# The start and the first passage between sets of a gated MLP kernel: DMAs on one queue, sums and casts in another order

## The chip, the cores and the metric

One core of a Trainium2 chip runs the kernel. TensorE (PE) multiplies, VectorE (DVE), ScalarE (ACT) and GpSimd (POOL) work on elements, SyncE (SP) issues DMAs, and so can ACT and POOL. Each of them runs its own instructions in order and waits on semaphores. The metric is the time of one execution in microseconds (us). Shorter is better.

## The reference

```python
# x [16, 256, 512], w1 [512, 4096], w2 [2048, 512], all float32
h = x @ w1
gate, value = np.split(h, 2, axis=-1)
h = np.maximum(gate, 0) * value
return (h @ w2).astype(np.float32)
```

That is two matrix products on 4096 rows, with a gate (columns 0 to 2047 of the first product) and a value (columns 2048 to 4095) between them.

## The kernel before

All products run in float16 with float32 accumulation. A small judge on the data's size decides whether this fast way's output stands or a general float32 way (a branch) runs. The branch isn't taken here, and the profile shows the fast way alone.

**Sets and blocks.** The 4096 rows are worked in four *sets* (s = 0 to 3) of 1024 rows, two halves of 512. A set's first product is made in 16 *blocks* (jb) of 128 hidden columns, gate and value together. Its second product, `mm2`, follows as a stream of 224 matmuls, of which the first 20 are put between the last matmuls of block 15 and the last 8 between the first blocks of the next set.

**Seven products instead of eight.** Each block is a 2x2 product of matrices of halves, made in Winograd's form of Strassen's scheme: seven products P1 to P7 on the quarters and on sums of quarters, at the cost of adding beforehand. Three families of sums are needed.
- *Of x*: x_S1 to x_S4 from x_A1 and x_A2 (the halves of a set's rows, transposed). DVE makes them (`x_sum`, line 448).
- *Of the weights*: T1 to T4. For w1 they are the tiles `wt`, one for each of six chunks of blocks (blocks 0-1, 2-3, 4-5, 6-7, 8-11, 12-15). POOL makes those of blocks 4 to 15 (`w1_ops`, line 158) while set 0 runs, DVE those of blocks 0 to 3 behind set 0's x sums, since set 0's blocks 0 to 3 are made in plain form (`Plain`). For w2 they are the tiles `v_T1` to `v_T4`: SP copies a quarter of w2 into each (line 529), and POOL then adds to it by an accumulating DMA (`add_w2`, line 161).
- *Of g*, the gated result of the first product: S1 to S4 (`g_sum`, line 271). S1 needs g's lower half of rows from block h and block h + 8, S3 needs blocks 0 to 7 only; S2 is made from S1, and S4 from S2. In set 0 POOL makes S3 at blocks 11 to 14, and three quarters of S1 after the last block; DVE makes the last quarter of S1, and S2 and S4. In later sets POOL makes one 512-wide piece after each block, and DVE the last two of each sum.

In `mm2` the order is P1 and P2 (from g itself) for three blocks of rows, and then P5 (S1), P6 (S2), P3 (S4), P7 (S3) and P4 (from g) for two of them, and so on. ACT and DVE evict: DVE's are lines 312 and 317.

**How x arrives.** Set 0's x is read by DMA: the first half as float32 on SP (tile `xf`, in the memory of g's S1), the second half as float16 on POOL (`xh`, in S2). TensorE transposes them. For sets 1 to 3 `cast_x(s)`, a DMA on POOL, writes the set's rows as float16 to DRAM (`x16`), and four DMA transposes on SP (line 384) bring them to x_A1 and x_A2. The tiles x_A exist once, so that the transposes wait for the last matmul that reads the set before, and for the cast. They and two fetches of plain rows for the judge are written behind a set's blocks, ahead of the output stores on the same queue.

**The start.** SP issues the two parts of x's first half (called x0 and x1 in the prediction), ACT the gate and the value part of w1's columns for blocks 0 and 1 (w0 and w1 there). ACT and DVE cast the latter to float16. A POOL copy into `gate` waits for x0 and holds back all of POOL's DMAs until then. POOL then fetches w1's columns of blocks 2 and 3, the second half of x, and the other columns. TensorE runs eight idle matmuls on a zeroed tile (`warm`) meanwhile.

Where the order is set: the program is written in the order in which each engine takes its instructions. For set 0 the list on POOL is, after the fetches, `w1_ops` with the fetches of w2 between them, the accumulates, and then what the loop over the time slots adds (`plan`, at block jb's product P1):

```python
if n == "P1" and s == 1 and jb < 2:
    cast_x(2 + jb)
...
if n == "P1" and s == 0 and jb in (11, 12, 13, 14):
    g_sum(nc.gpsimd, go, "S3", 2 * jb - 22, 2 * jb - 20)
    if jb == 12:
        add_w2("T4", "T2")
    if jb == 14:
        cast_x(1)
```

Of the kernel before, what the change touches and what calls it, by code (L numbers as in the profile page):

```python
# [9 lines left out]
F32, F32R, F16 = dt.float32, dt.float32r, dt.float16  # L10
# [6 lines left out]
P = 128  # L17
# [8 lines left out]
HALF = 256  # L26
NHC = 8
# [72 lines left out]
def fast_way(ctx, tc, x2, w1, w2, out2, flag):  # L100

    nc = tc.nc
# [5 lines left out]
    NJ = H // P  # L108
# [4 lines left out]
    wpool = ctx.enter_context(tc.tile_pool(name="wpool", bufs=1))  # L113
# [8 lines left out]
    w1_v = w1.rearrange("(e p) (g j) -> p e g j", p=P, g=2)  # L122
    w2_v = w2.rearrange("(hc p) n -> p hc n", p=P)
    x_v = x2.rearrange("(s b p) d -> s p b d", p=P, b=2 * NB)
# [4 lines left out]
    wr = [wpool.tile([P, 4, 2, n * P], F16, name=f"wr{c}") for c, (_, n) in enumerate(CHUNKS)]  # L129
    wt = [wpool.tile([P, 4, 2, n * P], F16, name=f"wt{c}") for c, (_, n) in enumerate(CHUNKS)]  # L130
    w2_h = [wpool.tile([P, NJ, HALF], F16, name=f"w2_{i}") for i in range(2)]
    v_t = {n: wpool.tile([P, NHC, HALF], F16, name=f"v_{n}") for n in ("T1", "T2", "T3", "T4")}
    x16 = {s: dpool.tile([SET, D], F16, name=f"x16_{s}") for s in range(1, NS)}

    NX = 2 * 2 * NB * NS
# [12 lines left out]
    V = {f"B{k + 1}{n + 1}": w2_h[n][:, k * NHC:(k + 1) * NHC] for k in range(2) for n in range(2)}  # L148
# [4 lines left out]
    def w1_ops(eng, jb, n):  # L153
        for t in TURNS:
            w1_one(eng, jb, n, *t)

    def w1_one(eng, jb, n, m, a, b, o):
        eng.tensor_tensor(W(m, jb, n), W(a, jb, n), W(b, jb, n), op=o)

    def add_w2(m, v):  # L160
        nc.gpsimd.dma_start(out=V[m], in_=V[v], accum_op=ADD)

    warm = tmp.tile([P, 2, TH], F32, name="warm", tag="tmp")
    warm_b = warm.rearrange("p a t -> p (a t)").bitcast(F16)
    nc.vector.memset(warm[:, 0], 0.0)
    ident = {t: wpool.tile([P, P], t, name=f"ident{k}") for k, t in enumerate((F32, F16))}
    gate = wpool.tile([P, 1], F32, name="gate")

# [5 lines left out]
    def x_tiles():  # L174
        o = {f"A{h}": xpool.tile([P, 4, TH], F16, name=f"x_A{h}") for h in (1, 2)}
        for h in (1, 2):
            for k in (1, 2):
                o[f"A{h}{k}"] = o[f"A{h}"][:, 2 * k - 2:2 * k]
        for n in ("S1", "S2", "S3", "S4"):
            o[n] = xpool.tile([P, 2, TH], F16, name=f"x_{n}")  # L180
        return o
# [86 lines left out]
    def g_sum(eng, go, n, h0, h1):  # L268
        for m, i0, i1, op in SUMS:
            if m == n:  # L270
                eng.tensor_tensor(go[n][:, h0:h1], go[i0][:, h0:h1], go[i1][:, h0:h1], op=op)  # L271
# [69 lines left out]
    def advance(stream, n):  # L341
        for _ in range(n):
            if stream is None or next(stream, 0) == 0:
                return
# [5 lines left out]
    def fetch_w2(i):  # L350
        ks, n = slice(i // 2 * NHC, i // 2 * NHC + NHC), i % 2
        nc.gpsimd.dma_start(out=w2_h[n][:, ks], in_=w2_v[:, ks, n * HALF:(n + 1) * HALF])

    def cast_x(s):
        nc.gpsimd.dma_start(out=x16[s], in_=x2[s * SET:(s + 1) * SET, :])

    def g_tiles():
        g = gpool.tile([P, NJ, SET], F16, name="g")
        gs = {n: gpool.tile([P, NHC, TH], F16, name=f"g_{n}") for n in ("S1", "S2", "S3", "S4")}
        return g, g_ops(g, gs)  # L360

    g, go = g_tiles()
    xf = go["S1"].rearrange("p a t -> p (a t)").bitcast(F32).rearrange("p (b d) -> p b d", b=NB)
    xh = go["S2"][:, :NB]
    wl = g[:, NJ - 4:].rearrange("p a t -> p (a t)").bitcast(F32).rearrange("p (e g j) -> p e g j", e=4, g=2)
# [16 lines left out]
    def turn_by_dma(s, o, h):  # L382
        for k in range(2):
            nc.sync.dma_start_transpose(out=o[f"A{h + 1}{k + 1}"], in_=x16[s][h * TH:(h + 1) * TH, k * 256:k * 256 + 256])
# [7 lines left out]
    def fetch_rows(s, q):  # L392
        rows[s, q] = xpool.tile([P, 2, D], F16, name=f"xn{q % 2}")
        nc.sync.dma_start(out=rows[s, q], in_=x16[s][q * 256:(q + 1) * 256].rearrange("(b p) d -> p b d", p=P))
# [3 lines left out]
        t = rows[s, b // 2][:, b % 2] if s else (xf, xh)[b // NB][:, b % NB]  # L398
        look(t[:, i % 2 * 256:i % 2 * 256 + 256], 4 * NB * s + i, 256)

    for b in (0, 2):
        nc.sync.dma_start(out=xf[:, b:b + 2], in_=x_v[0, :, b:b + 2])
    for g_ in range(2):
        nc.scalar.dma_start(out=wl[:, :, g_], in_=w1_v[:, :, g_, :2 * P])
    for t in ident.values():
        make_identity(nc, t)
    nc.gpsimd.tensor_copy(out=gate, in_=xf[:, 0, :1])
# [38 lines left out]
    def x_sum(o):  # L446
        n, i0, i1, op = sums.pop(0)
        nc.vector.tensor_tensor(o[n], o[i0], o[i1], op=op)
# [16 lines left out]
    def look_w1(i):  # L465
        c, o = place[i // 2 * 2]
        look(wr[c][:, :, i % 2, o * P:(o + 2) * P], NX + i, 1024)

    def look_w2(i):
        look(w2_h[i % 2][:, i // 2 * 4:i // 2 * 4 + 4].rearrange("p h n -> p (h n)"), NW + i, 1024)  # L470
# [26 lines left out]
    for s in range(NS - 1):  # L497
        for i in range(8):
            f = (lambda i=i + 8 * s: look_w1(i)) if s < 2 else (lambda i=i: look_w2(i))
# [11 lines left out]
    for s in range(NS):  # L511
        if s:
            g, go = g_tiles()
        first = NPLAIN if s == 0 else 0
        blocks = {jb: Block(xo, g, jb) for jb in range(first, NJ)}
        plan = {jb * PERIOD + at: (jb, n) for jb in blocks for n, at in SLOT.items()}
        last = NJ * PERIOD
        stream = mm2_stream(s, go)
        if s == 0:
            w1_ops(nc.gpsimd, 4, 2)  # L520
            fetch_w2(0)
            fetch_w2(1)
            w1_ops(nc.gpsimd, 6, 2)
            fetch_w2(2)
            fetch_w2(3)
            w1_ops(nc.gpsimd, 8, 2)
            w1_ops(nc.gpsimd, 10, 2)
            for m, v in (("T1", "B11"), ("T3", "B12"), ("T2", "B22"), ("T4", "B21")):
                nc.sync.dma_start(out=V[m], in_=V[v])
            for t in TURNS:  # L530
                w1_one(nc.gpsimd, 12, 4, *t)
                if t[0] == "T2":
                    add_w2("T1", "B12")
                    add_w2("T3", "B22")
            add_w2("T2", "T1")
        for at in range(first * PERIOD, last + PERIOD):
            if at in plan:
                jb, n = plan[at]
                if n == "P1" and s == 1 and jb < 2:
                    cast_x(2 + jb)  # L540
                if n == "P1" and s and jb in (4, 8):
                    fetch_rows(s, 1 + jb // 4)
                if n == "P1" and s == 0 and jb in (11, 12, 13, 14):
                    g_sum(nc.gpsimd, go, "S3", 2 * jb - 22, 2 * jb - 20)
                    if jb == 12:
                        add_w2("T4", "T2")
                    if jb == 14:
                        cast_x(1)
                getattr(blocks[jb], n)()
                if n == "P5":  # L550
                    for f in LOOKS.get((s, jb), ()):
                        f()
                if n == "P4" and s:
                    if jb < NHC:
                        g_sum(nc.gpsimd, go, "S3", jb, jb + 1)
                    elif jb < NJ - BY_DVE:
                        for m in ("S1", "S2", "S4"):
                            g_sum(nc.gpsimd, go, m, jb - NHC, jb - NHC + 1)
            elif at >= last:
                advance(stream, 4)  # L560
            else:
                advance(prev, 4)
        if s == 0:
            for h in (0, 2, 4):
                g_sum(nc.gpsimd, go, "S1", h, h + 2)
            g_sum(nc.vector, go, "S1", 6, 8)
            for m in ("S2", "S4"):
                for h in (0, NHC // 2):
                    g_sum(nc.vector, go, m, h, h + NHC // 2)
        else:  # L570
            for m in ("S1", "S2", "S4"):
                g_sum(nc.vector, go, m, NHC - BY_DVE, NHC)
        done = 20
        if s + 1 < NS:
            xo = x_tiles()
            for h in range(2):
                turn_by_dma(s + 1, xo, h)
            for q in range(2):
                fetch_rows(s + 1, q)
            advance(stream, 100)  # L580
            sums = list(SUMS)
            for _ in SUMS:
                x_sum(xo)
            if s == 0:
                w1_ops(nc.vector, 0, 2)
                w1_ops(nc.vector, 2, 2)
            advance(stream, MM2 - TAIL - 100 - done)
        else:
            advance(stream, MM2)
        prev = stream  # L590
# [29 lines left out]
```

## Time and profile before

| | us |
|---|---|
| median of 3 runs (lowest, highest) | 324.63 (324.35, 325.35) |
| the profiled execution | 325.27 |
| its span, first to last instruction | 323.5 |
| TensorE busy | 305.7 |
| DVE busy | 211.5 |
| ACT busy | 189.2 |
| POOL busy | 151.5 |

A row of the order of time has the start in us from the span's begin, the length in us, the engine, the line of the kernel, the operation, what it writes and reads (tiles by name, buffer numbers left out, so that `g_S` is any of g's sums and `x_S` any of x's), and how many instructions are merged. In brackets stands the engine's idle time before it, and what ended it. "SPq" and "POOLq" are DMA issues. A row of waits has the waiting engine and line, what it waited for, the total us, the number and the longest. A row of windows has the stretch, the busy time of PE, its weight loads, DVE, ACT and POOL with their counts, the granted TensorE clock, the mean busy share of the 16 DMA engines, and GB/s. "PE" with one digit for each of 40 slices shows the busy share of each 8.09 us in tenths. "DMA to landing" is the time from issue to landing, shortest, median and longest of the DMAs of one line in a stretch.

### The profile page before, as it was taken

What the parts mean: (1) busy time and instruction counts of PE and PEld (TensorE: products, weight loads), DVE (VectorE), ACT (ScalarE), POOL (GpSimd) and SP (SyncE); (2) the same over time, 40 slices, a digit from 0 to 9 for tenths busy, and PEclk for the clock granted to TensorE, in tenths of its full rate; (3) what the DMA queues carried; (4) which work ended last, traced back from release to release, by engine and by line L of the source; (5) the groups of instructions that cost most, each with busy time, mean ns of one, the idle gap of its engine ahead of it and who ended that gap; (6) DMA issues with size and microseconds to landing.
All of it is one profiled execution on the core that took longest, in us unless ns stands there. A gap on an engine that the chain in (4) does not pass through costs nothing.

```text
span 323.5 us, 5143 instructions
## 1 busy us (share of the span) xinstructions
PE 305.7 (95%) x1867; PEld 183.0 (57%) x1867; DVE 211.5 (65%) x329; ACT 189.2 (58%) x450; POOL 151.5 (47%) x137
## 2 busy tenths in 40 slices
PE   6999999978929999999999999999999999999993
PEld 3654444557814444448885444447885444447882
DVE  1377888895074888887424888888324888888311
ACT  2347766536607676673866766763876766763230
POOL 3879999980000433897000434897000334898000
PEclk9999999999969999999999999999999999999997
DMA  7999979499951101006422101007422101000123
GB/s 240 179 202 204 230 217 213 78 197 195 169 221 65 33 2 32 0 3 131 136 104 88 32 0 34 0 0 116 149 99 97 32 2 32 0 2 0 67 79 120
DMA packets 33593, 30.74 MB, mean 95 GB/s; under 512 B 13888, under 2 KB 27968, under 8 KB 33472
## 3 DMA queue, kind: packets, MB, share of 16 engines
q0 software_dynamic: 10704, 11.54, 21.9%
q1 hardware_dynamic: 21664, 17.70, 18.2%
q10 hardware_dynamic: 1200, 1.18, 1.2%
q8 instruction: 15, 0.25, 0.3%
q14 instruction: 10, 0.08, 0.1%
HBM read 24.12 MB, written 11.53 MB: 110 GB/s over the span
## 4 chain that ended last, share of the span: by engine, by line
PE 69%; DVE 0%; ACT 0%; issue 0%
PE Y L200 19%; PE X L200 13%; PE W L200 13%; PE Y L282 11%; PE W L282 6%; PE X L282 6%; ACT pv L323 0%; DVE pv L317 0%; DVE o L312 0%; PE W L485 0%
## 5 line engine op out<-in xcount | busy, mean ns | idle before, releaser
L271 POOL TENSOR_TENSOR g_S<-g 128x512 f16<-128x512 f16 (+1 forms) x49 | 64.0, 1332 | 133.4 <-DVE g L237 131.4
L200 PEld LDWEIGHTS <-wt 128*128 128x128 f16 x480 | 46.9, 98 | 56.9 <-issue 4.1
L200 PE MATMUL X<-x_A,wr 128*128 128x512 f16 x240 | 71.7, 381 | 0.2 <-ACT Y L207 0.2
L200 PE MATMUL Y<-x_S,wt 128*128 128x512 f16 x240 | 71.4, 379 | 0.0
L227 DVE SCALAR_TENSOR_TENSOR cc<-W,pu 128x512 f32<-128x512 f32 x60 | 41.5, 692 | 37.2 <-ACT pu L221 36.4
L200 PEld LDWEIGHTS <-wr 128*128 128x128 f16 x360 | 35.1, 98 | 41.3 <-issue 0.5
L207 ACT COPY Y<-X 128x512 f32<-128x512 f32 x60 | 34.2, 570 | 39.4 <-PE X L200 21.4
L282 PEld LDWEIGHTS <-g_S 128*128 128x128 f16 x512 | 49.6, 98 | 9.5 <-DVE g_S L271 1.9
L282 PEld LDWEIGHTS <-g 128*128 128x128 f16 x384 | 37.9, 99 | 14.8 <-issue 6.5
L221 ACT ACTIVATE pu<-Y 128x512 f32<-128x512 f32 x60 | 35.9, 598 | 14.3 <-PE Y L200 14.3
L228 DVE SCALAR_TENSOR_TENSOR g<-X,cc 128x512 f16<-128x512 f32 x60 | 41.5, 691 | 2.3
L237 DVE SCALAR_TENSOR_TENSOR g<-Y,cc 128x512 f16<-128x512 f32 x60 | 40.9, 682 | 2.8 <-PE Y L200 2.8
L233 DVE SCALAR_TENSOR_TENSOR cc<-Y,pu 128x512 f32<-128x512 f32 x60 | 40.9, 681 | 0.1
L214 ACT ACTIVATE pu<-W 128x512 f32<-128x512 f32 x60 | 36.1, 602 | 0.1
L200 PE MATMUL W<-x_S,wt 128*128 128x512 f16 x120 | 36.0, 382 | 0.0
L200 PE MATMUL Y<-x_A,wt 128*128 128x512 f16 x120 | 35.5, 377 | 0.2 <-DVE cc L233 0.2
L200 PE MATMUL W<-x_S,wr 128*128 128x512 f16 x120 | 35.7, 379 | 0.0
L282 PE MATMUL Y<-v_T,g_S 128*128 128x256 f16 x256 | 30.8, 273 | 0.5 <-DVE g_S L271 0.5
L282 PE MATMUL X<-w,g 128*128 128x256 f16 x256 | 31.2, 272 | 0.0
L312 DVE SCALAR_TENSOR_TENSOR o<-W,pv 128x256 f32<-128x256 f32 x16 | 6.7, 424 | 31.6 <-PE W L282 31.6
L323 ACT ACTIVATE pv<-Y 128x256 f32<-128x256 f32 x16 | 6.1, 382 | 32.0 <-PE Y L282 32.0
L282 PE MATMUL Y<-v_T,g 128*128 128x256 f16 x128 | 17.1, 281 | 5.9 <-DVE pv L317 5.9
(67 smaller groups left out, 317.6 us busy)
## 6 DMA issues: line engine op xcount, KB each, us to landing
out_dram<-o SPq DMA_DIRECT2D x16, 256.0 KB, 2.2
out_dram<-pv SPq DMA_DIRECT2D x15, 256.0 KB, 2.0
x<-in_x_dram POOLq DMA_DIRECT2D x3, 1024.0 KB, 9.5
xn<-x SPq DMA_DIRECT2D x12, 256.0 KB, 3.0
wr<-in_w_dram POOLq DMA_DIRECT2D x4, 512.0 KB, 13.9
w<-in_w_dram POOLq DMA_DIRECT2D x4, 512.0 KB, 10.9
v_T<-w SPq DMA_DIRECT2D x4, 512.0 KB, 4.9
wr<-in_w_dram POOLq DMA_DIRECT2D x6, 256.0 KB, 8.6
```

The costliest lines, as they stand in the source:

```text
L200: nc.tensor.matmul(ps, W(wn, self.jb)[:, b], self.xo[xn][:, b, :], start=fresh and b == 0, stop=b == 1, skip_group_check=True)
L207: nc.scalar.copy(out=self.Y, in_=self.X)
L214: nc.scalar.activation(self.p5, self.W, COPY, scale=GS)
L221: nc.scalar.activation(self.u2, self.Y, COPY, scale=-GS)
L227: nc.vector.scalar_tensor_tensor(out=self.c12, in0=self.W, scalar=GS, in1=self.u2, op0=MULT, op1=ADD)
L228: nc.vector.scalar_tensor_tensor(out=self.g[:, self.jb, :TH], in0=self.X, scalar=0.0, in1=self.c12, op0=MAX, op1=MULT)
L233: nc.vector.scalar_tensor_tensor(out=self.c22, in0=self.Y, scalar=-GS, in1=self.p5, op0=MULT, op1=ADD)
L237: nc.vector.scalar_tensor_tensor(out=self.g[:, self.jb, TH:], in0=self.Y, scalar=0.0, in1=self.c22, op0=MAX, op1=MULT)
L271: eng.tensor_tensor(go[n][:, h0:h1], go[i0][:, h0:h1], go[i1][:, h0:h1], op=op)
L282: nc.tensor.matmul(ps, go[gn][:, k, b * P:(b + 1) * P], V[vn][:, k, :], start=fresh and k == 0, stop=k == NHC - 1, skip_group_check=True)
L312: nc.vector.scalar_tensor_tensor(out=d["o1"][:, HALF:], in0=d["W"], scalar=1 / GS, in1=d["pu"][:, 1], op0=MULT, op1=ADD)
L323: nc.scalar.activation(d["o2"][:, :HALF], d["Y"], COPY, scale=1 / GS)
```

## The change

It has five parts.
- *Start.* SP issues all four first DMAs, in turn: x0, w0, x1, w1. The idle tile's zeroing is half as wide.
- *w2's sums.* T3 and T2 become the halves of one tile `v_12`. One 1 MB copy from `w2_h[1]` (B12 and B22 side by side) takes the place of two of 0.5 MB, so that SP issues three copies instead of four. T4's accumulate goes from block 12 to block 15.
- *cast_x(1)* goes from block 14 to the place right behind T2's accumulate, ahead of all sums of g.
- *Sums of g in set 0.* POOL makes pieces of S1 and S3 in turn at blocks 11 and 13, and a piece of S1 at block 15. The second half of S3 moves from POOL to the end of DVE's list.
- *Casts of sets 2 and 3* go from set 1's blocks 0 and 1 (P1) to the places behind POOL's S3 pieces of set 1's blocks 1 and 4, which wait for these blocks.

```diff
-    v_t = {n: wpool.tile([P, NHC, HALF], F16, name=f"v_{n}") for n in ("T1", "T2", "T3", "T4")}
+    v_12 = wpool.tile([P, NJ, HALF], F16, name="v_12")
+    v_t = {n: wpool.tile([P, NHC, HALF], F16, name=f"v_{n}") for n in ("T1", "T4")}
+    v_t.update(T3=v_12[:, :NHC], T2=v_12[:, NHC:])
...
-    nc.vector.memset(warm[:, 0], 0.0)
+    nc.vector.memset(warm[:, 0, :HALF], 0.0)
...
-    for b in (0, 2):
-        nc.sync.dma_start(out=xf[:, b:b + 2], in_=x_v[0, :, b:b + 2])
-    for g_ in range(2):
-        nc.scalar.dma_start(out=wl[:, :, g_], in_=w1_v[:, :, g_, :2 * P])
+    for i in range(2):
+        nc.sync.dma_start(out=xf[:, 2 * i:2 * i + 2], in_=x_v[0, :, 2 * i:2 * i + 2])
+        nc.sync.dma_start(out=wl[:, :, i], in_=w1_v[:, :, i, :2 * P])
...
-            for m, v in (("T1", "B11"), ("T3", "B12"), ("T2", "B22"), ("T4", "B21")):
-                nc.sync.dma_start(out=V[m], in_=V[v])
+            for to, v in ((V["T1"], V["B11"]), (v_12, w2_h[1]), (V["T4"], V["B21"])):
+                nc.sync.dma_start(out=to, in_=v)
...
             add_w2("T2", "T1")
+            cast_x(1)
...
-                if n == "P1" and s == 1 and jb < 2:
-                    cast_x(2 + jb)
...
-                if n == "P1" and s == 0 and jb in (11, 12, 13, 14):
-                    g_sum(nc.gpsimd, go, "S3", 2 * jb - 22, 2 * jb - 20)
-                    if jb == 12:
+                if n == "P1" and s == 0 and jb in (11, 13, 15):
+                    h = jb - 11
+                    if h == 4:
                         add_w2("T4", "T2")
-                    if jb == 14:
-                        cast_x(1)
+                    for m in ("S1", "S3")[:2 - h // 4]:
+                        g_sum(nc.gpsimd, go, m, h, h + 2)
...
                         g_sum(nc.gpsimd, go, "S3", jb, jb + 1)
+                        if s == 1 and jb in (1, 4):
+                            cast_x(2 + jb // 4)
...
-            for h in (0, 2, 4):
-                g_sum(nc.gpsimd, go, "S1", h, h + 2)
             g_sum(nc.vector, go, "S1", 6, 8)
             for m in ("S2", "S4"):
                 for h in (0, NHC // 2):
                     g_sum(nc.vector, go, m, h, h + NHC // 2)
+            g_sum(nc.vector, go, "S3", NHC // 2, NHC)
```

POOL's instructions from the accumulates of w2's sums to the end of set 0 and the first of set 1, before. Here `v_T3` etc. are w2's sums, `w2_1` is `w2_h[1]`, `wt5` and `wr5` are w1's sums and raw columns of blocks 12 to 15, `x16_s` what a cast writes, and the number at a name's end a buffer:

```order
L161 DMA v_T3_100<-w2_1_97 128x2048
L158 TENSOR_TENSOR wt5_95<-wr5_89 128x1024
L158 TENSOR_TENSOR wt5_95<-wr5_89,wt5_95 128x1024
L161 DMA v_T2_99<-v_T1_98 128x2048
L271 TENSOR_TENSOR g_S3_114<-g_111 128x1024 x2
L161 DMA v_T4_101<-v_T2_99 128x2048
L271 TENSOR_TENSOR g_S3_114<-g_111 128x1024 x2
L355 DMA x16_1_102<-in_x_dram 32x16384
L271 TENSOR_TENSOR g_S1_112<-g_111 128x1024 x3
L355 DMA x16_2_103<-in_x_dram 32x16384
L355 DMA x16_3_104<-in_x_dram 32x16384
L271 TENSOR_TENSOR g_S3_1051<-g_1048 128x512 x8
```

And with the change:

```order
L160 TENSOR_TENSOR wt5_95<-wr5_89,wt5_95 128x1024
L163 DMA v_12_98<-v_T1_99 128x2048
L357 DMA x16_1_101<-in_x_dram 32x16384
L273 TENSOR_TENSOR g_S1_111<-g_110 128x1024
L273 TENSOR_TENSOR g_S3_113<-g_110 128x1024
L273 TENSOR_TENSOR g_S1_111<-g_110 128x1024
L273 TENSOR_TENSOR g_S3_113<-g_110 128x1024
L163 DMA v_T4_100<-v_12_98 128x2048
L273 TENSOR_TENSOR g_S1_111<-g_110 128x1024
L273 TENSOR_TENSOR g_S3_1048<-g_1045 128x512 x2
L357 DMA x16_2_102<-in_x_dram 32x16384
L273 TENSOR_TENSOR g_S3_1048<-g_1045 128x512 x3
```

The cast of set 1 now stands ahead of every g sum, S1 and S3 take turns with T4's accumulate ahead of the last piece, and two pieces of S3 are gone; the casts of sets 2 and 3 stand behind two and five pieces of set 1's S3.

SP's queue from its first DMA to set 1's transposes, before:

```order
L402 DMA g_S1_112<-in_x_dram 128x2x512 x2
L529 DMA v_T1_98<-w2_0_96 128x2048
L529 DMA v_T3_100<-w2_1_97 128x2048
L529 DMA v_T2_99<-w2_1_97 128x2048
L529 DMA v_T4_101<-w2_0_96 128x2048
L384 DMA_TRANSPOSE x_A1_763<-x16_1_102 128x2x512 x2
L384 DMA_TRANSPOSE x_A2_764<-x16_1_102 128x2x512 x2
```

And with the change, where `g_110` is the memory in g that holds the float32 columns of w1:

```order
L404 DMA g_S1_111<-in_x_dram 128x2x512
L405 DMA g_110<-in_w1_dram 128x4x256
L404 DMA g_S1_111<-in_x_dram 128x2x512
L405 DMA g_110<-in_w1_dram 128x4x256
L530 DMA v_T1_99<-w2_0_96 128x2048
L530 DMA v_12_98<-w2_1_97 128x4096
L530 DMA v_T4_100<-w2_0_96 128x2048
L386 DMA_TRANSPOSE x_A1_760<-x16_1_101 128x2x512 x2
L386 DMA_TRANSPOSE x_A2_761<-x16_1_101 128x2x512 x2
```

The two DMAs of w1's first columns have come from ACT's queue between those of x, and the second copy is twice as long and needs both of `w2_h[1]`'s fetches.

## The prediction

> **What bounds the kernel now.** I read the page first, then the waits, then the order of time around the one place where TensorE stands still.
>
> ```profile
> PE 305.7 (95%) x1867; PEld 183.0 (57%) x1867; DVE 211.5 (65%) x329; ACT 189.2 (58%) x450; POOL 151.5 (47%) x137
> PE   6999999978929999999999999999999999999993
> ```
>
> TensorE (PE) is the bound, and whatever the change wins must come out of the few slices below 9: the start, and slices 9 to 12 (65 to 97 us), which are the passage from set 0 to set 1. The waits name what it waited for there, the second fence on SP's queue:
>
> ```profile
> PE Y L282 <- DVE pv L317: 5.9, 1, 5.9
> DVE x_S L448 <- DMA x_A<-x: 9.2, 1, 9.2
> ```
> ```profile
> SPq L384 <- DMA x<-in_x_dram: 26.3, 1, 26.3
> ```
>
> The order of time shows the chain behind them (start, length, engine, line):
>
> ```profile
> 62.21 1.03 PE L282 MATMUL X<-w,g 128*128 128x256 f16 x8
> 63.30 0.81 POOL L355 DMA_DIRECT2D x<-in_x_dram  x1
> 63.87 6.52 POOL L271 TENSOR_TENSOR g_S<-g 128x1024 f16<-128x1024 f16 x3
> 66.19 4.76 DVE L271 TENSOR_TENSOR g_S<-g 128x1024 f16<-128x1024 f16 x1
> 68.32 0.60 PE L282 MATMUL W<-v_T,g_S 128*128 128x256 f16 x4
> 70.09 1.25 POOL L355 DMA_DIRECT2D x<-in_x_dram  x2
> 70.45 0.39 PE L282 MATMUL W<-v_T,g_S 128*128 128x256 f16 x2 [1.53 <-POOL g_S L271]
> 70.87 2.35 DVE L271 TENSOR_TENSOR g_S<-g_S,g 128x2048 f16<-128x2048 f16 x2
> 72.96 13.27 SPq L384 DMA_TRANSPOSE x_A<-x  x4
> 88.39 0.69 DVE L448 TENSOR_TENSOR x_S<-x_A 128x1024 f16<-128x1024 f16 x1 [9.15 <-DMA x_A<-x]
> 95.12 1.86 PE L282 MATMUL Y<-v_T,g 128*128 128x256 f16 x8 [5.86 <-DVE pv L317]
> ```
>
> The casts' landing, in us from issue (the first of them took the 9.5):
>
> ```profile
> DMA to landing us min/median/max: 7.9/9.5/12.7
> ```
>
> There are two separate stalls. **First:** PE wants S1 at 68.32, but POOL makes it only from 63.87 to 70.39, and DVE's own piece takes 4.76 us. **Second:** cast_x(1) is issued at 63.30 and lands 9.5 us later, at 72.8; only then do the transposes start, beside the casts of sets 2 and 3 (issued at 70.09). x_A lands at 88.39. DVE has been waiting for it since 79.2, with the output evictions queued behind, and PE stops until 95.12. It then runs on a cold clock:
>
> ```profile
> 93.00:96.00 3.00, 0.88 (x5) 0.61 (x5) 2.40 (x7) 0.00 (x0) 0.00 (x0) 0.50 0.25 92
> ```
>
> (Third column from the right: granted clock 0.50.) What the passage costs in all is read against the next one, which has neither stall:
>
> ```profile
> 145.07 6.93 SPq L384 DMA_TRANSPOSE x_A<-x  x4
> 146.19 1.03 PE L282 MATMUL X<-w,g 128*128 128x256 f16 x8
> 169.76 1.04 PE L282 MATMUL Y<-v_T,g 128*128 128x256 f16 x8
> 219.29 0.93 PE L282 MATMUL X<-w,g 128*128 128x256 f16 x7
> ```
>
> From the second product's first matmul of one set to that of the next: 219.29 - 146.19 = 73.10 us undisturbed, 146.19 - 62.21 = 83.98 us for set 0. So 10.88 us, idle time and cold clock together, is the most that the passage can give. Shifting the undisturbed rows by 83.98 gives PE's due times without the stalls: the P4 that came at 95.12 is due at 85.78.
>
> **The change, part by part.** (1) *The copies of w2's parts and POOL's order.* Rows, SP, POOL, PE:
>
> ```profile
> 45.40 1.11 SPq L529 DMA_DIRECT2D v_T<-w  x2
> 46.53 1.86 POOL L161 DMA_DIRECT2D v_T<-w  x2
> 47.76 2.79 POOL L158 TENSOR_TENSOR wt<-wr 128x1024 f16<-128x1024 f16 x1
> 49.84 2.78 POOL L158 TENSOR_TENSOR wt<-wr,wt 128x1024 f16<-128x1024 f16 x1
> 53.63 0.59 PE L200 MATMUL Y<-x_S,wt 128*128 128x512 f16 x2
> 55.70 0.59 PE L200 MATMUL Y<-x_A,wt 128*128 128x512 f16 x2 [0.18 <-DVE cc L233]
> ```
> ```profile
> DMA to landing us min/median/max: 2.9/4.9/6.5
> DMA to landing us min/median/max: 2.9/3.3/3.7
> ```
>
> The last two rows are SP's four copies, and the two of 45.40 alone. T3's accumulate, the second of POOL's two from 46.53 (at 47.2), now waits for the whole 1 MB copy into v_12, which waits for w2's last fetch (45.40 here). The two 0.5 MB copies issued from 45.40 landed in 2.9 and 3.7 us, the second at 49.6; without T3's earlier copy the fetch should be about a us sooner. I take v_12 at 48.7, so POOL is D = 1.5 us late (ends: 0.5, and 2.4 at 49.6). Queued behind it are T3 and T4 for blocks 12 to 15, ready at 50.55 and 52.62 now and wanted by PE at 53.63 and 55.70: 3.1 us of cover, so D costs PE nothing.
>
> (2) *The cast.* It moves ahead of all S sums, right behind T2's accumulate: 52.6 + 0.6 + 1.5 = 54.7. It has the accumulates of T3 and T2 ahead of it on its queue, so 9.5 us is the least; I take landing at 65 (ends 64.3, and 67.5 with the longest landing). The undisturbed transposes of the next passage, issue in ns and landing in us:
>
> ```profile
> L384 SPq DMA_TRANSPOSE x_A<-x x4: 1226/1266/1297, 145.1 to 150.7; - x4
> DMA to landing us min/median/max: 3.1/3.3/3.7
> ```
>
> x_A1 is free from 145.07 - 83.98 = 61.1, x_A2 soon after, both before the cast lands. Then four transposes are three issues of 1.27 us and a landing of 3.7, 7.5 us; T4's accumulate, now issued at 64, may cost them 3. So x_A lands at 72.5 to 78, say 75.5. From x_A to PE's stalled P4 took 95.12 - 88.39 = 6.73 us, so anything up to 85.78 - 6.73 = 79.05 is hidden. The second stall goes, with its cold clock.
>
> (3) *The S sums.* POOL's take 6.52 / 3 = 2.17 us each. S1, S3, S1, S3 from 55.4 end at 64.1, T4's accumulate is issued (0.6), the fifth sum ends at 66.9. DVE's S1 piece stood for 4.76 us while POOL ran its sums and ended 0.56 us after them (70.95 against 70.39). So S1 is whole at 67.5. PE's due times go by the undisturbed passage's chain of waits, where two blocks of rows, 16 matmuls, take 1.75 us in each product:
>
> ```profile
> 166.43 1.75 PE W L282 x16
> ```
>
> From 68.32 on, DVE's quarter of S1 is wanted at 68.98 (after 6 matmuls). Then on DVE at 1.18 each (2.35 / 2): S2 68.6 and 69.8 (wanted 70.05 and 70.5), S4 71.0 and 72.2 (71.8 and 72.24), the added S3 half 73.3 (74.0). All in time, the last by little; I charge 0.2 us. With D = 2.4 the S4 half is 0.9 late.
>
> (4) *Casts 2 and 3* now go behind set 1's S3 sums 1 and 4. Set 1's 16 blocks lie between 95.12 and 145.07, some 3.1 us each, so the casts are out about 44 and 34 us before the transposes of 145.07 that read the first of them, and land in 12.7 at most: nothing. Each holds POOL's next sum by 0.8 us (the row of 63.30), and POOL has one sum of half the size of (3) per block there, so a block makes it good. The smaller memset frees PE 0.2 us sooner for idle matmuls: nothing.
>
> (5) *The start.* In the windows the last two columns are the DMA share and GB/s:
>
> ```profile
> 2.00:4.00 2.00, 2.00 (x6) 0.71 (x5) 0.00 (x0) 1.17 (x1) 0.00 (x0) 1.00 0.68 186
> 4.00:8.00 4.00, 2.67 (x11) 1.71 (x10) 0.83 (x2) 0.62 (x1) 1.61 (x3) 1.00 1.07 385
> ```
> ```profile
> 6.48 1.94 PE L371 MATMUL W<-ident,g_S 128*128 128x128 f32 x8 [1.33 <-DMA g_S<-in_x_dram]
> 9.43 0.45 DVE L388 CAST wr<-g 128x512 f16<-128x512 f32 x1 [1.14 <-DMA g<-in_w_dram]
> ```
> ```profile
> 8.19 1.44 POOL L411 DMA_DIRECT2D g_S<-in_x_dram  x2
> 15.90 0.50 PE L379 MATMUL X<-ident,g_S 128*128 128x128 f16 x6
> ```
> ```profile
> DMA to landing us min/median/max: 7.1/7.4/7.7
> ```
>
> x0 and w0, 1.05 MB on two queues, had moved by 5.8 at these rates and landed at 6.4. Alone and first, x0's 0.52 MB has moved by 4.4: landing at 5.0, w0 still 6.4, x1 7.7, w1 9.4 as before, last in the row. PE's first transposes start 1.4 us earlier, and the first products 1.1 or more, since w0's cast on DVE, which stands ahead of the eviction of those transposes, has its data at about the same time as now. But PE next needs the second x half, which landed at 8.19 + 7.1 = 15.3, 0.6 before PE took it at 15.90; POOL asks for it earlier now (its gate is x0), through the same busy DMA engines. I take a gain of 0.5 (ends: 1.1 gained; 0.3 lost, below).
>
> The Trainium skill ("DMA: Bandwidth & Descriptors", sections "Issuing engines are not separate DMA queues" and "Queues, rings and completion order") says that queues share the same 16 DMA engines, that each engine takes turns between queues packet by packet, and that issuing from more engines saves only issue time. By that rule x0 does get the whole rate at first, but POOL's fetches, opened earlier, then take turns with w1, the last of the row; what this would give is the second rival below. No run yet shows it.
>
> **Sum.** Passage 10.88 - 0.2 = 10.7, start 0.5: 11.2 us. The profiled execution took 325.27 us (span 323.5 and 1.8 around it): 314.1. It lies 0.64 above the median of 324.63, so against that median 313.4; I say 313.5. The forecast's own range is 312.5 to 314.5.
>
> **Rivals.** *S sums still late:* v_12 lands at 49.6 to 51, POOL ends at 68 to 69 and DVE's seven pieces run behind PE: 0.9 to 2.5 us are left of the first stall instead of 0.2, 314.1 to 315.7. For it: the S4 half has no slack; against: the copies' landing rows.
>
> *The start loses:* POOL's fetches begin at about 7 instead of 8.2, halve the rate of w1's last 0.6 MB, and w1 lands at 10.7. How much of this 1.3 us PE's own work covers isn't seen: between all of it and none, the middle, with the 0.5 gain gone, is a loss of 0.3: 314.2.
>
> *x_A late:* the cast waits out both accumulates on its queue and lands at 69 to 71, or the transposes take the 15.4 us that they took here (72.96 to 88.39): x_A at 80.5 to 82, a stall of 1.5 to 3 and up to 1 us of cold clock: 314.9 to 317.4. Against: two casts ran beside them here, now one accumulate.
>
> *No change:* x_A lands near 88 again, for a reason that I can't see.
>
> *Slower:* the 1 MB copy. If it moves at the rate of the slowest of SP's four 0.5 MB copies (6.5 us, beside fetches), it lands 13 us later, at 58.4; blocks 12 to 15 wait for T3, PE loses 58.4 - 50.3 = 8.1, the S sums slip by 2.5 more, and 324.0 is left. It turns the sign when the copy lands after 59, and at 62 gives 327.6. For it: nothing else was queued so deep on one landing; against: 2.9 and 3.7 us at that very place.
>
> **Chances.** Forecast 58%, S sums late 14%, start loses 13%, x_A late 11%, no change 2%, slower 2%. 0.3% (1.0 us) is about what a measurement of this kernel tells from no change; the first four cases are all faster by more: 0.96, then 0.02 and 0.02. The range, 312.3 to 317.0, takes in the first three cases and most of the fourth.
>
> **What would show it.** Right: the second product of set 0 starts at about 62 and set 1's at about 135.5, 73 to 74 apart; the wait of PE for pv and of DVE for x_A is gone; the transposes start near 65 and last about 7 us. Wrong: POOL waiting for the v copy beyond 50.3, PE waiting on g_S after 70, or TensorE's clock at 0.50 near 90 as before; for the start, the second x half's transposes on PE later than 15.9.

## The result and the profile after

The changed kernel takes 313.69 us (median of 4, 313.49 to 313.96); the kernel before took 324.99 beside it. The ratio is 0.965, with a 95% interval of 0.962 to 0.968. Forecast were 313.5 us, and 312.3 to 317.0 as the range. The profiled execution took 313.77 us with a span of 312.0.

From the page, TensorE's share and its slices:

```profile
PE 302.4 (97%) x1867; PEld 182.0 (58%) x1867; DVE 209.4 (67%) x330; ACT 188.9 (61%) x450; POOL 147.7 (47%) x135
PE   7799999999999999999999999999999999999993
```

The digits below 9 at slices 9 to 12 are gone; what is left is the start and the end. The order of time in the passage from set 0 to set 1 (line numbers are those of the changed kernel, two or so higher than before):

```profile
54.48 1.15 POOL L357 DMA_DIRECT2D x<-in_x_dram  x1
61.49 1.03 PE L284 MATMUL X<-w,g 128*128 128x256 f16 x8
64.00 3.02 POOL L273 TENSOR_TENSOR g_S<-g 128x1024 f16<-128x1024 f16 x1
64.62 8.49 SPq L386 DMA_TRANSPOSE x_A<-x  x4
65.46 2.12 DVE L273 TENSOR_TENSOR g_S<-g 128x1024 f16<-128x1024 f16 x1
67.59 1.91 PE L284 MATMUL W<-v_T,g_S 128*128 128x256 f16 x16
72.17 1.48 PE L284 MATMUL W<-w,g_S 128*128 128x256 f16 x12 [0.35 <-DVE g_S L273]
75.78 0.68 DVE L449 TENSOR_TENSOR x_S<-x_A 128x1024 f16<-128x1024 f16 x1
85.72 1.04 PE L284 MATMUL Y<-v_T,g 128*128 128x256 f16 x8
135.25 1.04 PE L284 MATMUL X<-w,g 128*128 128x256 f16 x8
208.35 1.03 PE L284 MATMUL X<-w,g 128*128 128x256 f16 x8
```

The cast goes out at 54.48 and has landed by 64.6, when the transposes start. S1 is there before PE gets to it (16 matmuls in one run at 67.59). DVE takes its x sums at 75.78 without a wait (no bracket), and P4, which had stood until 95.12, comes at 85.72. From set 0's second product to set 1's it is 135.25 - 61.49 = 73.76 us instead of 83.98, and to set 2's again 73.10. TensorE idles 0.35 us in this stretch (columns: the stretch, its length, PE's busy time):

```profile
61.00:96.00 35.00, 34.65 (x271) 26.21 (x270) 24.83 (x40) 21.96 (x52) 7.17 (x5) 1.00 0.59 136
```

So 83.98 - 73.76 = 10.22 us come from the passage, and 62.21 - 61.49 = 0.72 from what lies ahead of it. The last store is issued 10.94 us sooner (307.59 against 318.53); another 0.56 of the span's 11.5 lies behind that issue, a stretch of 4.4 us here and 5.0 before, and of 4.0 to 5.1 in other runs with the change or most of it, so that it isn't put down to the change.

The start:

```profile
4.67 1.39 PE L373 MATMUL W<-ident,g_S 128*128 128x128 f32 x8
7.30 1.03 PE L257 MATMUL X<-x_A,wr 128*128 128x256 f16 x8 [0.80 <-DVE x_A L375]
9.43 0.76 DVE L390 CAST wr<-g 128x512 f16<-128x512 f32 x1 [2.28 <-DMA g<-in_w_dram]
10.83 1.03 PE L257 MATMUL W<-x_A,wr 128*128 128x256 f16 x8 [1.61 <-DVE x_A L375]
15.18 0.61 PE L381 MATMUL X<-ident,g_S 128*128 128x128 f16 x8
```

PE's first transposes come 1.8 us sooner, and the first products too; then PE waits 1.61 us for an eviction that stands on DVE behind the cast of w1's second part, which still lands at 9.4.

### The profile page after: what moved, and what is told of

Its sections match the earlier page's. It is cut to its first block, busy times and chain, and to the rows that moved or that the text cites. A ratio compares the mean times of both kernels' runs of the same rounds, so it can differ in the third digit from the quotient of the medians.

```text
span 312.0 us, 5142 instructions
## 1 busy us (share of the span) xinstructions
PE 302.4 (97%) x1867; PEld 182.0 (58%) x1867; DVE 209.4 (67%) x330; ACT 188.9 (61%) x450; POOL 147.7 (47%) x135
## 4 chain that ended last, share of the span: by engine, by line
PE 91%; DVE 3%; DMA 2%; issue 1%; ACT 1%; SPq 0%; DVEq 0%
PE Y L202 25%; PE X L202 16%; PE W L202 16%; PE Y L284 13%; PE W L284 8%; PE X L284 8%; DMA g<-in_w_dram 2%; PE W L257 2%; PE X L257 2%; DVE g_S L273 1%; DVE g L239 0%; ACT x_A L382 0%; SPq L404 0%; DVE wr L390 0%; DVE cc L229 0%
## 5 line engine op out<-in xcount | busy, mean ns | idle before, releaser
L273 POOL TENSOR_TENSOR g_S<-g 128x512 f16<-128x512 f16 (+1 forms) x47 | 60.6, 1331 | 125.8 <-DVE g L239 123.8
L284 PE MATMUL Y<-v,g_S 128*128 128x256 f16 x256 | 30.7, 273 | 0.0
L273 POOL TENSOR_TENSOR g_S<-g,g_S 128x512 f16<-128x512 f16 x18 | 21.8, 1211 | 1.4
L273 POOL TENSOR_TENSOR g_S<-g_S,g 128x512 f16<-128x512 f16 x18 | 20.8, 1157 | 1.4
```

The lines of the kernel that those rows point to most:

```text
L284: nc.tensor.matmul(ps, go[gn][:, k, b * P:(b + 1) * P], V[vn][:, k, :], start=fresh and k == 0, stop=k == NHC - 1, skip_group_check=True)
```

## Experiments

The passage is given below as the time from set 0's second product to set 1's; undisturbed it is 73.10 us. The ratio is to the kernel before, run beside it.

| kernel | median us | ratio (95% interval) | begin of the second product | passage |
|---|---|---|---|---|
| before | 324.99 | 1 | 62.21 | 83.98 |
| changed | 313.69 | 0.965 (0.962 to 0.968) | 61.49 | 73.76 |
| start alone | 324.74 | 0.997 (0.995 to 0.999) | 61.34 | 84.40 |
| casts held alone | 317.18 | 0.974 (0.970 to 0.979) | 62.38 | 75.93 |
| sums of g alone | 324.02 | 0.994 (0.992 to 0.997) | 61.27 | 83.84 |
| changed, both casts not held | 322.90 | 0.991 (0.988 to 0.994) | 61.33 | 83.50 |
| changed, one cast not held | 315.20 | 0.969 (0.964 to 0.973) | 61.44 | 75.52 |
| changed, set 1's cast late | 315.87 | 0.971 (0.965 to 0.977) | 60.81 | 77.37 |
| changed, four copies of w2 | 313.24 | 0.964 (0.960 to 0.967) | 61.37 | 73.08 |
| changed, eviction ahead of cast | 313.42 | 0.964 (0.960 to 0.967) | 61.06 | 74.03 |
| changed, run again | 313.69 | 0.964 (0.962 to 0.966) | 60.75 | 74.03 |
| changed, start of before | 314.42 | 0.966 (0.964 to 0.968) | 61.20 | 74.28 |
| four copies and eviction first | 313.65 | 0.964 (0.962 to 0.966) | 61.62 | 73.09 |
| four copies and POOL's gate on w0 | 313.93 | 0.964 (0.961 to 0.967) | 61.45 | 73.10 |

**Only the casts of sets 2 and 3 held back**, in the kernel before.

```diff
-                if n == "P1" and s == 1 and jb < 2:
-                    cast_x(2 + jb)
...
                         g_sum(nc.gpsimd, go, "S3", jb, jb + 1)
+                        if s == 1 and jb in (1, 4):
+                            cast_x(2 + jb // 4)
```

> The kernel before with only the casts of sets 2 and 3 held back (behind set 1's S3 pieces of blocks 1 and 4). Theory A: the cast of set 1 still lands at 72.8, but the transposes run without casts beside them, 7.5 us instead of 15.4, and x_A is there at 80.4. The first stall (S1 sums) stays and puts the P4 that stalled at about 85.8 + 3.3 = 89.1, so x_A is wanted at 82.4 and the second stall is gone whole: passage 3.3 us over 73.10 instead of 10.88, about 317.4. Rival B: the transposes take 15 us at this place whatever runs beside them (the output stores, the tail of POOL's list): x_A near 88 again, about 325.

317.18 us: this part alone takes 8 of the 11 us. The transposes are short and DVE doesn't wait for them, though the cast of set 1 is as late as before:

```profile
70.98 5.46 SPq L384 DMA_TRANSPOSE x_A<-x  x4
78.86 0.68 DVE L448 TENSOR_TENSOR x_S<-x_A 128x1024 f16<-128x1024 f16 x1
138.31 1.04 PE L282 MATMUL X<-w,g 128*128 128x256 f16 x8
```

The passage keeps 75.93 - 73.10 = 2.83 us, which is the first stall. Rival B falls.

**The change without holding the casts back.**

```diff
+                if n == "P1" and s == 1 and jb < 2:
+                    cast_x(2 + jb)
...
-                        if s == 1 and jb in (1, 4):
-                            cast_x(2 + jb // 4)
```

> The changed kernel with the casts of sets 2 and 3 put back to where they were (issued right behind POOL's last sum, near 67). Theory A: they run beside the transposes from about 69 on, which makes x_A 4 to 7 us later than the 75.6 of the changed kernel, 80 to 83 against about 79 where it starts to cost: 315 to 318.5, say 316.5. Rival B: the early cast of set 1 does all the work and holding the others back does none: 313.7.

322.90 us, above both. The sign of theory A holds, its size is missed by 6 us. The casts are issued at 66.24 and 66.8, and the last transpose waits for both:

```profile
64.81 18.35 SPq L386 DMA_TRANSPOSE x_A<-x  x4
66.24 1.94 POOL L357 DMA_DIRECT2D x<-in_x_dram  x2
86.29 0.69 DVE L449 TENSOR_TENSOR x_S<-x_A 128x1024 f16<-128x1024 f16 x1 [10.23 <-DMA x_A<-x]
93.01 1.87 PE L284 MATMUL Y<-v_T,g 128*128 128x256 f16 x8 [6.94 <-DVE pv L319]
```
```profile
DMA to landing us min/median/max: 10.5/12.9/15.3
```

The last cast lands at 66.8 + 15.3 = 82.1, and SP issued the last transpose at 81.9. x_A is there at 86.2, 10.6 us later than in the changed kernel, and PE stalls 6.94 us and starts cold (eight matmuls in 1.87 us instead of 1.04). So the early cast of set 1 is worth next to nothing while the others run beside its transposes: the passage is 83.50 us, against 83.84 in the sums-alone kernel below, whose cast goes out at 62.85.

**One cast not held** (the cast of set 2 at block 0 of set 1, that of set 3 as changed).

> The changed kernel with the cast of set 2 alone put back behind POOL's last sum of set 0 (issued near 66); the cast of set 3 stays held. So far: with no cast beside them the four transposes had x_A there at 75.6 (issued from 64.6), with both casts at 86.2, and in every run with both casts SP issued the last transpose within 1.3 us of the last cast's landing. Theory A (the transposes wait out whatever casts are in flight): one cast costs half of it, x_A at 80 to 81.5, which is 1.5 to 3 us past where it starts to cost, with some cold clock: 315.5 to 317.5. Rival B (two casts in flight together saturate something, one alone doesn't matter): 313.7 to 314.3.

315.20 us, x_A at 80.7, as theory A has it; the time lies a little under its range:

```profile
64.88 13.60 SPq L386 DMA_TRANSPOSE x_A<-x  x4
80.73 0.69 DVE L449 TENSOR_TENSOR x_S<-x_A 128x1024 f16<-128x1024 f16 x1 [4.65 <-DMA x_A<-x]
87.45 1.03 PE L284 MATMUL Y<-v_T,g 128*128 128x256 f16 x8 [1.35 <-DVE pv L319]
```

With none, one and two casts beside them x_A came at 75.6, 80.7 and 86.2: 5.1 and 5.5 us for each. From x_A to P4 it was 6.72 us here and in the run above, as in the kernel before (6.73), so what x_A costs starts at 85.72 - 6.73 = 79.0 in the changed kernel; 80.7 - 79.0 = 1.7, and the passage is 75.52 - 73.76 = 1.76 longer.

**Set 1's cast late** (behind POOL's fourth sum, the others held).

```diff
             add_w2("T2", "T1")
-            cast_x(1)
...
                     if h == 4:
+                        cast_x(1)
                         add_w2("T4", "T2")
```

> The changed kernel with the cast of set 1 behind POOL's fourth sum (issued near 63.5 instead of 54.5), all else as changed. Theory A: the cast lands at 71.5 to 73, the transposes take 7.5 to 9, x_A at 79.5 to 82 against 79: a stall of 0.5 to 3 us, 314.2 to 317, say 315.3. So the early cast is worth a fraction of the holding back. Rival B: the early cast is worth as much as the holding back (8 us): above 320.

315.87 us: theory A, about 2 us more than the changed kernel (the four runs, 314.33 to 317.30, all lie above it). There is another wait, that I hadn't foreseen: T4's accumulate stood behind the cast on POOL's queue, and PE waited for it.

```profile
62.54 1.10 POOL L357 DMA_DIRECT2D x<-in_x_dram  x1
74.13 5.47 SPq L386 DMA_TRANSPOSE x_A<-x  x4
76.22 1.92 PE L284 MATMUL Y<-v_T,g 128*128 128x256 f16 x16 [1.13 <-DMA v_T<-v]
81.94 0.69 DVE L449 TENSOR_TENSOR x_S<-x_A 128x1024 f16<-128x1024 f16 x1 [6.39 <-DMA x_A<-x]
88.67 1.03 PE L284 MATMUL Y<-v_T,g 128*128 128x256 f16 x8 [1.79 <-DVE pv L319]
```

That wait of 1.13 us costs nothing in this trace, since P4 comes 6.73 us after x_A again: x_A alone is late, by 81.94 - 78.3 = 3.6 us (79.0 shifted by the 0.68 that the second product begins sooner here), and the passage is 77.37 - 73.76 = 3.61 longer. The cast took 11.5 us to land, where the kernel with the casts held alone, which issues it at 63.00, had it in 7.8. With 7.8 here too, and the 7.7 that the transposes took, x_A would have been there at 78.0, in time (an estimate from these rows). So the 2 us belong to the late cast with T4's accumulate right behind it; what the late place costs by itself no run shows.

**Only the sums of g**, in the kernel before.

> The kernel before with only the sums of g in the new order (S1 and S3 pieces in turn at blocks 11 and 13, a piece of S1 at block 15, half of S3 on DVE), the cast of set 1 about where it was (behind four sums, near 63), the casts of sets 2 and 3 behind POOL's last sum as before. Theory A: TensorE no longer waits for S1, but x_A comes as late as before, so the time won at 68 to 77 us is lost again in a longer wait at 89 to 95: 324 to 325.7, no change. Rival B: the two stalls add up, and the time falls by the first one's 2.5 to 3.3 us: about 322.

324.02 us. PE no longer waits for S1, and its second wait grows from 5.86 to 8.83 us:

```profile
6.44 1.06 PE L371 MATMUL W<-ident,g_S 128*128 128x128 f32 x8 [1.29 <-DMA g_S<-in_x_dram]
87.11 0.69 DVE L448 TENSOR_TENSOR x_S<-x_A 128x1024 f16<-128x1024 f16 x1 [12.13 <-DMA x_A<-x]
93.82 1.87 PE L282 MATMUL Y<-v_T,g 128*128 128x256 f16 x8 [8.83 <-DVE pv L317]
```

The passage is 83.84 us, as before (83.98): theory A. In this profile the begin is 0.9 us sooner, though its start is that of before; the first row shows why, and the last section comes back to it. The time's 0.6% is more than theory A's nothing. x_A came 1.3 us sooner, as the two casts were issued near 65.5 instead of 70.1.

**Only the start**, in the kernel before.

> The kernel before with the start of the change alone (the four first DMAs on SP in turn, and the narrower memset). In the changed kernel TensorE reached the transposes of the second x half 0.72 us sooner (15.90 to 15.18) and POOL ran its list 1.3 us sooner (first accumulate 46.53 to 45.20), since its fetches open with x0. Theory A: the passage is still set by x_A, which hangs on POOL's list (the cast of set 1) and not on TensorE, so the time falls by POOL's 1.3 us: about 323.6. Rival B: the time falls by TensorE's own 0.7 us: about 324.2. Rival C: the start wins nothing once the passage stalls as before: 324.9.

324.74 us, 0.3% (0.1 to 0.5%) less than the kernel before, or 0.3 to 1.6 us: more than C's nothing, but A's 1.3 and B's 0.7 both lie within it. x_A and the stalled P4 did come POOL's 1.25 us sooner (P4 at 93.87), but set 1's second product began only 0.45 us sooner (145.74 against 146.19). The granted clock (third column from the right) in the stretch that follows, of this kernel and of the one before, is low for longer:

```profile
96.00:99.00 3.00, 3.00 (x11) 1.38 (x10) 0.00 (x0) 1.72 (x5) 0.00 (x0) 0.55 0.23 87
```
```profile
96.00:99.00 3.00, 3.00 (x14) 1.59 (x13) 0.00 (x0) 1.36 (x3) 0.00 (x0) 0.62 0.45 169
```

**The change without the start.**

> The changed kernel with the start of before (w1's first columns on ACT's queue, full memset). Theory A: TensorE begins the second product 0 to 0.9 us later (62.2 to 62.4 where the clock was still at half rate at the first transposes, 61.3 where it was not), and POOL, whose fetches open 1.9 us later, runs its list 1.3 us later, so that S2 and S4 come later still: 0.5 to 1.5 us more than the changed kernel, 314.7. Rival B: the start is worth nothing by itself and the passage absorbs POOL's delay: equal to the changed kernel within 0.2.

314.42 us against 313.69 of the changed kernel run beside it: within theory A's range, but the intervals of the two ratios overlap, so a worth of the start in the changed kernel of more than nothing isn't settled by the times. In the profile the begin is 61.20, no later than with the new start, and the passage 74.28.

**Four copies of w2's parts** (the tiles and copies of before, all else as changed).

> The changed kernel with the four copies of w2's parts of before instead of the 1 MB copy into one tile. Theory A: the copies lie off the path in both forms (POOL waited 3.0 us for the one copy, but T3 and T4 of blocks 12 to 15 came before TensorE wanted them): 313.4 to 314.0; POOL's list runs up to 1.5 us sooner, so at most the last 0.3 us of waiting for S4 go. Rival B: the copy is part of the gain, since it leaves the fetches more of the DMA engines: 314.2 or more.

313.24 us, theory A; its trace shows more than I expected:

```profile
61.37 1.04 PE L282 MATMUL X<-w,g 128*128 128x256 f16 x8
134.45 1.04 PE L282 MATMUL X<-w,g 128*128 128x256 f16 x8
```

The passage is 73.08 us, all that there is to win, against 73.76 to 74.28 in the four profiles that keep the one copy and both stalls away (changed, changed again, eviction first, start of before). So the one copy costs 0.7 to 1.2 us in the passage by delaying POOL's list; the times, 313.24 against 313.69, point the same way, but weren't taken beside each other and don't settle it.

**The eviction ahead of the cast of w1's second part**, on DVE and ACT.

```diff
-    cast_w(1)
     turn_pair(xo, 2)
+    cast_w(1)
```

> The changed kernel with the eviction of the second pair of x transposes written ahead of the cast of w1's second part, on DVE and ACT. In the changed kernel TensorE waited 1.6 us, to 10.83, for an eviction (10.11 on DVE) that stood behind the cast of w1's second part, which landed at 9.43. Theory A: the eviction goes at 8.9 to 9.6, the cast at 9.6 to 10.1, and TensorE goes on at 10.1 to 10.2: 0.6 to 0.7 us less, 313.0. Rival B: the second x half, which landed at about 13.9 and is wanted at 14.5 then, or POOL's weight sums hold TensorE back next, and it is 313.6.

313.42 us, between the two theories and within the changed kernel's own spread.

**The changed kernel again**, beside the next two.

> The changed kernel once more, beside the next two on the same chip: 313.4 to 314.0.

313.69 us, the same median; the begin is 60.75 and the passage 74.03.

**Both together.**

> The changed kernel with w2's four copies of before and the eviction ahead of the cast of w1's second part. With the four copies alone the passage took 73.08 us, no more than an undisturbed one (the changed kernel 73.76), and the swap let TensorE begin the second product 0.2 to 0.4 us sooner. Theory A: both add up, 0.8 to 1.1 us under the changed kernel beside it: 312.7. Rival B: an earlier TensorE only waits longer for S2 and S4 in the passage: 313.2.

313.65 us, level with the changed kernel beside it (313.69): both theories miss. The passage is 73.09 as with the four copies, but the second product begins at 61.62, since w1's second part was cast only from 9.97 in that profile, now behind the evictions, and PE waited for that cast instead.

**POOL's gate on w0**, with the four copies.

```diff
-    nc.gpsimd.tensor_copy(out=gate, in_=xf[:, 0, :1])
+    nc.gpsimd.tensor_copy(out=gate, in_=wl[:, 0, 0, :1])
```

> The changed kernel with w2's four copies of before, and with POOL's gate on w0 instead of x0: POOL's own fetches open when w0 has landed (near 6.1) and not when x0 has (near 4.5). So far, with the new start, TensorE's second group of products has waited for w1's second part, which landed at 9.0 to 9.7 in all the traces, although x's two parts were there by 8. Theory A (w1 shares the DMA engines with POOL's early fetches): w1 lands at 8.2 to 8.7 now, TensorE goes on 0.6 us sooner (second group at 9.6 to 10.0, second product's first matmul at 60.4 to 60.8 instead of 60.8 to 61.5), and POOL's list, 1.3 us later, is still in time without the one big copy: 312.7. Rival B (w1 comes last at the DMA engines' full rate, whatever POOL does): w1 at 9.0 or later, 313.3 as with the four copies alone, or more where POOL's delay shows.

313.93 us, rival B: POOL's fetches open at 6.6 instead of 4.6, and w1's second part still comes at 9.65.

```profile
9.65 0.43 DVE L388 CAST wr<-g 128x512 f16<-128x512 f32 x1 [2.43 <-DMA g<-in_w_dram]
```

This alone doesn't clear POOL's fetches, since the gate hardly moved their traffic: by the packets, POOL's queue begins to move data near 7.9 in the changed kernel, though its first fetch is issued at 4.59, and near 8.3 here. But up to 8 the four first DMAs have the engines to themselves in both kernels, and have moved 1.95 and 1.92 of their 2.10 MB by then. So w1 comes last because it stands last among 2.1 MB; whether POOL's fetches hold up the last 0.15 to 0.18 MB, from 8 to about 9, isn't separated. None of these kernels is clearly faster than the changed one.

## Why the prediction was right, and where not

The median, 313.69, lies 0.2 us from the forecast, and of its terms the passage carries: 10.7 forecast, 10.22 measured. That it came so close is partly luck: the passage gave 0.48 us less than its term, the start 0.22 more, and 0.56 lie behind the last store's issue, in no term at all. By its steps:

- *Sign and place.* The two stalls, and 10.88 us as the most that the passage can give, held: the four-copy kernels reach 73.08 to 73.10, all of it. What the prediction didn't say is how unequal the parts are. Holding the casts alone gives 8 us, the sums alone next to nothing, since the second stall waits for a landing and takes back what the first gives up, and the late cast of set 1 costs some 2 us, in a run that has T4's accumulate right behind it.
- *(1) The copies.* The last fetch was two us sooner, not one (the copy is issued at 43.39), but the 1 MB copy took 5.2 us to land, not 4.3. POOL waited for it until 49.16:

```profile
43.39 0.47 SPq L530 DMA_DIRECT2D v<-w  x1
49.16 0.88 POOL L163 DMA_DIRECT2D v<-w  x1 [3.02 <-DMA v<-w]
54.98 0.59 PE L202 MATMUL Y<-x_A,wt 128*128 128x512 f16 x2 [0.18 <-DVE cc L235]
```

  POOL's delay D was 1.9 us there (1.5 forecast) and 2.6 against PE, which was 0.7 us ahead; POOL's next two sums took 2.45 and 2.43 us instead of 2.8, so that only 1.2 of it were left at T2's accumulate (53.90 against 52.74). Block 12 didn't wait for it (the last row has the same 0.18 as before).
- *(2) The cast and the transposes.* Issue 54.48 (54.7), landing by 64.6 (65), x_A at 75.6 (75.5). The transposes took 11.0 us, that is the 7.5 of undisturbed ones and 3.5 more, put down to T4's accumulate (3 forecast), which landed at 69.6, 5.0 us into them. With no accumulate beside them they took 7.6 us (the casts held alone: 70.98 to 78.6), and 9.8 in the four-copy kernel, where it landed 3.1 us into them; no run moves the accumulate by itself. The due time worked out for x_A, 79.05, came out at 79.0, but by two misses that cancel: PE began 0.72 us sooner and lost 0.66 on the way.
- *(3) The sums.* POOL's last ended at 67.0 (66.9) and DVE's piece of S1 at 67.6 (67.5). S4 was whole at 72.1 (72.2). So the sums came when forecast, and yet PE waited 0.35 us for S4, and in all 0.66 us of the passage were left, where 0.2 were charged: the due times had been taken from the old begin of 62.21, without the start's own gain, and PE was 0.72 us ahead of them. The rival "S sums still late" asked for v_12 at 49.6 or later and gave 0.9 us or more; v_12 landed at 48.6. The four-copy kernels, whose POOL sums end 1.6 to 2.6 us sooner, have nothing left.
- *(4)* cost nothing: the passages from set 1 on are 73.10 in both kernels.
- *(5) The start* is the step that came out close for the wrong reason: 0.72 measured, 0.5 forecast. x0 landed 3.6 us after its issue (at 4.5, not 5.0). The second x half, said to hold PE back at 15.3, had landed (its first part) at 13.7, 1.5 us before PE took it at 15.18. What held PE was w1's second part, behind whose cast an eviction stood (1.61 us). How much of the 0.72 is the start's own, one pair of profiles can't say: in two others the old start began the second product at 61.20 and 61.27, and 61.49 is no gain on these (last section).

The rule of the Trainium skill ("DMA: Bandwidth & Descriptors", "Issuing engines are not separate DMA queues"), from which the rival "the start loses" was made, agrees with x0's early landing (4.5, against 6.4 beside w0 on a second queue). The rival itself, POOL's fetches taking the rate from w1, didn't come about up to 8 us: POOL's queue had moved two packets by then. One queue and two moved about the same, 325 and 318 GB/s from 2 to 8 us.

Whether the end of w1's second part, from 8 to about 9, is held up by POOL's fetches stays open.

## What to carry to other kernels

Where several stalls stand in one passage, work out for each the due time at which it begins to cost, and look which one waits for a landing: taking away an earlier stall only lengthens that wait, and an early issue is worth nothing while other transfers stand in its way. Bulk transfers that nobody needs soon go behind the landing that somebody does need; tying them to a later result on their own queue is enough. A later passage of the same work in the same profile gives the most that a change can win, before any term is worked out.

## What the runs showed of the hardware

*Transposes wait out casts.* In every run with both casts in flight SP issued the last of four DMA transposes within 1.3 us of the last cast's landing, whenever the first was issued: 84.1 against 83.3 in the kernel before, 81.9 against 82.1 with set 1's cast early, 82.4 against 81.3 with the sums alone, 83.0 against 81.8 with the start alone. The four took 7.6 us with no cast or accumulate beside them, 15 to 21 with two casts. In these runs the transposes that were issued behind the casts landed behind the last of them. One that was issued ahead of them, at 64.81 in the run with set 1's cast early, landed in 7.7 us, as the first one does in the changed kernel (7.5), while the casts were still in flight. So it looks like the order of issue; by what rule of the queues, the runs don't show.

*The first transposes take either of two lengths, by chance.* The same code and the same landing gave the first eight transposes in 1.94 us (the kernel before) or in 1.06 (the row of the sums-alone kernel). The column of the granted clock reads 1.00 there in both, so that the clock as the cause is read from the lengths alone. With the start of before the second product began at 62.21 and 62.38 in the two profiles with the long ones, at 61.27 and 61.20 in the two with the short. With the new start it began between 60.75 and 61.62 in ten profiles, whichever it was (1.04 to 1.91 us), as w1's landing sets the time there (DVE casts its second part at 9.02 and 9.03 where the begin is 60.75 and 60.81, and at 9.4 to 10.0 in the others). The Trainium skill ("TensorE: Matmul & The Clock Gate", "What's actually happening") says that the clock is raised after a busy window of about 3.4 us, and that the window runs freely and doesn't begin with the kernel; the two lengths agree with that, while no run here shows the window itself. So in these profiles the new start wins about a microsecond over the old one's long kind and nothing over its short one.

*DVE and POOL on sums.* DVE's quarter of S1 took 2.12 us and POOL's last sum 3.02 where they met (65.46 and 64.00 above), against 2.17 for POOL's sum before. In the kernel before, DVE's piece arrived during the second of three POOL sums and was done only after the third (66.19 to 70.95, POOL's third to 70.39), though such a piece takes DVE 0.69 us alone, as in the four-copy kernel: it didn't run between the second and the third.
